# Moving side work out of two PSUM banks, and more projections ahead of the first scores, in the recurrent stage of a hybrid decoder step

## The chip, the cores and the metric

One core of a Trainium2 chip runs the kernel. The metric is the device time of one execution in microseconds; the median of the runs shown is 2340.65 us.

## What is computed

One layer of a decoder trunk serves 2048 prompt tokens and 32 sample tokens (8 sequences of 4). RMSNorm is followed by one input projection (1024 columns in, 5912 out). Branch A is sparse attention with three gated parts. Branch B is a gated linear recurrence in four heads with keys and values of 128. Both are gated, projected, merged, and added to the input. The change touches branch B alone, which is, per head and chunk:

```python
G = cumsum(log f)
o_inter = (q * exp(G)) @ S
A[t, s] = sum_d q[t, d] * exp(G[t, d] - G[s, d]) * k[s, d]      # s <= t
o = o_inter + A @ v
S = exp(G_last) * S + (k * exp(G_last - G)).T @ v
...
o = o * rsqrt(mean(o * o) + eps) * norm_g * silu(z)
```

The prompt starts from S = 0; each sample sequence has a state of its own, which is read and written back.

## The kernel before

**Projections.** `make_projections` (line 269) walks through groups of 256 columns: compressed, selected and window keys and values, then q, f, qb, ib, zb, z, ma and mb. For each group `load_w` (line 298) fetches the weights, takes their largest magnitude on VectorE (line 302), has TensorE transpose the 128 maxima of the partitions into one row of a PSUM bank (`pow2_scale`, line 197), reduces that row on VectorE (line 199), and splits the scaled weights into two 16-bit halves (lines 308 and 309). That bank is the tile `tp`, one buffer. A feature group then takes 24 matmuls for each chunk of up to 512 tokens (line 399) into one of two banks `ps`, which ScalarE and VectorE evacuate (lines 415 to 421); the late mb groups do the same at line 459 with ScalarE alone. The projections are a generator. `fill(ns)` adds to a credit and lets it emit work until the credit is used up, six matmuls of n columns costing 2.52 * n ns.

**The recurrent stage.** `hgrn` (line 645) handles 32 units, 8 chunks of 256 tokens by 4 heads, and is a generator too: `along(hgrn(), 1200.0)` runs it step by step, and after each `yield` comes `fill(1200)`. Its PSUM pools are `pa` (two banks `p4` for the scores) and `po` with one bank each of `pk`, `pu` and `ov`; with two banks of `ps` and one of `tp` all eight are given out. For a unit, `factors` loads its inputs and makes exponentials (ScalarE, VectorE, GpSimd); `scores` transposes a factor into `pk` (line 781) and multiplies the score blocks into `p4` (line 802), at high priority; `values` multiplies the chunk's contribution to the state into `pu` (line 825), the outputs into `ov` (lines 829 and 831), and VectorE makes the new state from `pu` (lines 834 and 836). When the four heads of a chunk are done, their outputs are normalized, and in each of the next four units one of them is scaled (`gate_scale`, line 683) and passes through `gate_out` (line 685): two transposes into `ov` (line 688), a multiply by the gate on VectorE that reads `ov` (line 691), a split into halves and two stores. The order in a unit's step is: scaling, factors of the unit after next, scores of the next one, gated output, values.

From the seventh unit on a step of `sample_heads` (line 849) follows each unit. A head of the samples multiplies scores into `pk` (line 873), outputs into `pu` (lines 878 and 880), transposes a factor into `pk` (line 884), and makes two products of four states each into `pu` (line 891), from which VectorE updates the states (line 896), four instructions for each product. Line 670 takes the output gates' largest magnitude through `ov` once, before the first unit.

**What sets the order.** The framework gives every instruction a priority by its place in the program, estimates times, and writes one fixed list for each engine before the run; an engine works off its list in order. Tiles of one name share the buffers of that name. Waits between engines on a buffer are semaphores that it inserts. Ahead of the loop stands the start of the stage:

```python
            ahead = [factors(*units[0])]
            for _ in range(6):
                yield
            ahead.append(factors(*units[1]))
            yield
            yield from scores(ahead[0])
```

Of the kernel before, what the change touches and what calls it, by code (L numbers as in the profile page):

```python
# [10 lines left out]
F32 = mybir.dt.float32  # L11
# [129 lines left out]
def trunk_kernel(ctx: ExitStack, tc: tile.TileContext, A, O):  # L141
# [503 lines left out]
    def hgrn():  # L645
        with ExitStack() as st:
# [3 lines left out]
            po = st.enter_context(tc.tile_pool(name="hpo", bufs=1, space=PSUM, side="right"))  # L650
# [23 lines left out]
            def rsqrt(ss):  # L674
                n = ss.shape[0]
                ve.tensor_scalar(ss, ss, 1.0 / 128, EPS, op0=OP.mult, op1=OP.add)
                y = hp.tile([128, 8], F32, name="rsy", bufs=3)[:n, :ss.shape[1]]
                ve.tensor_scalar(y, near_rsqrt(ss, hp), sob[:n], 9.0 / 64, op0=OP.mult, op1=OP.mult)
                return y

            def gate_scale(o_sb, y, nt):

                ve.tensor_tensor(o_sb, o_sb, y[:, :, None].to_broadcast([128, nt, 128]), op=OP.mult)

            def gate_out(o_sb, zt, nt, place):
                pt = po.tile([128, 512], F32, name="ov")
                for j in range(nt):
                    pe.transpose(pt[:, j * 128:j * 128 + 128], o_sb[:, j], ident)
                n = nt * 128
                g = zt  # L690
                ve.tensor_mul(g[:, :n], pt[:, :n], zt[:, :n])
                gh = hp.tile([128, NC], F16, name="gh", bufs=1)
                gl = hp.tile([128, NC], F16, name="gl", bufs=1)
                ac.activation(gh[:, :n], g[:, :n], AF.Copy)
                ve.tensor_sub(gl[:, :n], g[:, :n], gh[:, :n])
                for d, x in ((obh_d, gh), (obl_d, gl)):
                    to, x = place(d, x)
                    sy.dma_start(to, x)
# [54 lines left out]
            def factors(c, h):  # L753
                t0 = c * NC
                G, qt, kt, Bq, Bk, Xo, Kd, eG = common(h, t0, NC, 128)
                v = hp.tile([128, NJ, 128], F32, name="v", bufs=3)
                sy.dma_start(v, ib_d[t0:t0 + NC, h * 128:(h + 1) * 128].rearrange("(j p) e -> p j e", p=128))
                Xs = []
                for li, L in enumerate(LEVELS):
                    nb = NC // (2 * L)  # L760
                    Gv = G.rearrange("p (b i) -> p b i", i=2 * L)
                    ref = Gv[:, :, L - 1:L].to_broadcast([128, nb, 2 * L])
                    X = hp.tile([128, NC], F32, name=f"X{li}")
                    Xv = X.rearrange("p (b i) -> p b i", i=2 * L)

                    if nb == 2:
                        for b in range(2):
                            ac.activation(Xv[:, b], Gv[:, b], AF.Abs, scale=-1.0, bias=Gv[:, b, L - 1:L])
                    else:
                        ve.tensor_tensor(Xv, Gv, ref, op=OP.subtract)  # L770
                        ac.activation(X, X, AF.Abs)
                    ac.activation(X, X, AF.Exp, scale=-1.0)
                    gp.tensor_mul(Xv[:, :, :L], Xv[:, :, :L], kt.rearrange("p (b i) -> p b i", i=2 * L)[:, :, :L])
                    gp.tensor_mul(Xv[:, :, L:], Xv[:, :, L:], qt.rearrange("p (b i) -> p b i", i=2 * L)[:, :, L:])
                    Xs.append(X)
                return dict(Bq=Bq, Bk=Bk, Xo=Xo, Kd=Kd, eG=eG, v=v, Xs=Xs, c=c, h=h)
# [72 lines left out]
            def sample_heads():  # L849

                def zeros(name, shape):
                    t_ = hc.tile([128] + shape, F32, name=name)
                    gp.memset(t_, 0.0)
                    return t_

                for nm in ("Bk", "Kd"):
                    WIDE[nm] = zeros(nm + "_s", [128])
                v_, AT_, kd_, vm_ = zeros("vs_", [128]), zeros("ATs", [32]), zeros("kd_s", [128]), zeros("vm", [4, 128])

                oT = hc.tile([128, 4, 32], F32, name="oT")  # L860
                for h in range(4):
                    G, qt, kt, Bq, Bk, Xo, Kd, eG = common(h, 2048, 32, 4)
                    v = v_[:32]
                    sy.dma_start(v, ib_d[2048:2080, h * 128:(h + 1) * 128])
                    S0 = hp.tile([128, 8, 128], F32, name="S0", bufs=1)
                    sy.dma_start(S0, A["state_hgrn"][0, :, h].rearrange("b d e -> d b e"))

                    def masked(b2):
                        ve.tensor_tensor(vm_[:32], v[:, None].to_broadcast([32, 4, 128]), bd[:, 4 * b2:4 * b2 + 4, None].to_broadcast([32, 4, 128]), op=OP.mult)

                    masked(0)
                    pb = po.tile([128, 512], F32, name="pk")
                    mm(pb[:, :32], WIDE["Bk"], Bq, True, True)
                    AT = AT_[:32]
                    ve.tensor_mul(AT, pb[:32, :32], lm4[:32, 3])
                    yield
                    ov = po.tile([128, 512], F32, name="pu")[:, :32]
                    mm(ov, v_, AT_, True, False)
                    for b in range(8):
                        mm(ov[:, 4 * b:4 * b + 4], S0[:, b], Xo[:, 4 * b:4 * b + 4], False, True)  # L880
                    ve.tensor_copy(oT[:, h], ov)
                    yield
                    pk = po.tile([128, 512], F32, name="pk").rearrange("p (a b) -> p a b", a=4)
                    pe.transpose(pk[:, 0], WIDE["Kd"], ident)
                    kd = kd_[:32]
                    ve.tensor_copy(kd, pk[:32, 0])
                    yield
                    Sn = S0
                    for b2 in range(2):
                        pu = po.tile([128, 512], F32, name="pu").rearrange("p (a b) -> p a b", a=4)  # L890
                        mm(pu, kd_, vm_, True, True)
                        if b2 == 0:
                            masked(1)
                        for b in range(4):
                            bb = 4 * b2 + b
                            ve.scalar_tensor_tensor(Sn[:, bb], S0[:, bb], eG[:, bb:bb + 1], pu[:, b], op0=OP.mult, op1=OP.add)
                        if b2 == 0:
                            yield
                    sy.dma_start(O["s_hgrn"][0, :, h].rearrange("b d e -> d b e"), Sn)
                    yield  # L900
                pt = po.tile([128, 512], F32, name="pk")
                pe.transpose(pt[:, :128], oT.rearrange("p h t -> p (h t)"), ident)
                o_sb = hp.tile([128, NJ, 128], F32, name="o_sb", bufs=5)[:, :1]
                ss = hp.tile([128, 4 * NJ], F32, name="ss")[:, :1]
                ac.activation(o_sb[:, 0], pt[:, :128], AF.Copy)
                jk = hp.tile([128, 128], BF, name="jk", bufs=1)
                ac.activation(jk, pt[:, :128], AF.Square, accum_out=ss)
                zt = hp.tile([128, NC], F32, name="zt", bufs=6)

                def place(d, x):  # L910
                    return d[:, 2048:2080].rearrange("(h p) t -> p h t", p=128), x[:, :128].rearrange("p (h t) -> p h t", t=32)

                sy.dma_start(*place(zb_d, zt)[::-1])
                yield
                gate_scale(o_sb, rsqrt(ss), 1)
                yield
                gate_out(o_sb, zt, 1, place)

            beside = sample_heads()
            units = [(c, h) for c in range(NP // NC) for h in range(4)]  # L920

            ahead = [factors(*units[0])]
            for _ in range(6):
                yield
            ahead.append(factors(*units[1]))
            yield
# [3 lines left out]
            def gated(step):  # L930

                if ready:
                    o_sb, zt, y, h2, c2 = ready[0]
                    if step == 0:
                        gate_scale(o_sb, y, NJ)
                    else:
                        gate_out(o_sb, zt, NJ, lambda d, x: (d[h2 * 128:(h2 + 1) * 128, c2 * NC:(c2 + 1) * NC], x))
                        ready.pop(0)
# [1159 lines left out]
    with ExitStack() as s2:  # L2098
        sw, sb = ExitStack(), ExitStack()
        load_x, fill, state = make_projections(s2, sw, sb)  # L2100
# [18 lines left out]
        attention_operands(s2, att)  # L2119
        fill(0, ("zb", 2))  # L2120
        along(hgrn(), 1200.0)
        fill(0, ("z", 2))
        fill(350.0)
# [38 lines left out]
```

## Time and profile before

| | |
|---|---|
| median of the runs | 2340.65 us (2339.75 to 2341.35) |
| the profiled execution | 2322.12 us |
| its span, first to last instruction | 2320.2 us |
| its mean granted TensorE clock | 0.99 |

The trace is of one execution. Instructions are on their engines: PE is TensorE, DVE VectorE, ACT ScalarE, POOL GpSimd. Busy time counts a matmul from start to modelled end, and matmuls overlap, so TensorE's idle time says more than its busy time. A wait is charged to the instruction that stood still and to what the trace shows as ending it; "issue" means that it shows nothing.

### The profile page before, as it was taken

The page shows a single profiled execution, that of the slowest core. Times are in us where ns is not written, and L with a number is a line of the kernel's source. Part 1 is how long each engine was busy: PE and PEld are TensorE (multiplying, and loading weights), DVE is VectorE, ACT ScalarE, POOL GpSimd, SP SyncE. Part 2 cuts the span into 40 slices and gives each one's busy share as a digit, 9 for nine tenths or more (in the row PEclk, how much of TensorE's full clock was granted, in tenths as well). Part 3 has the DMA queues.
Part 4 walks back from the last instruction along what each step waited for, and adds up shares of the span by engine and source line. Part 5 has one row for each costly group of instructions (what it writes and reads, how often), then busy time and mean ns, then how long its engine had stood idle before and what let it go on. Part 6 is the DMA issues. An engine that isn't in the chain of part 4 may idle for free.

```text
span 2320.2 us, 57026 instructions
## 1 busy us (share of the span) xinstructions
PE 2215.4 (95%) x22427; PEld 1537.1 (66%) x22427; DVE 1490.3 (64%) x3780; ACT 1191.0 (51%) x2658; POOL 1005.6 (43%) x1190
## 2 busy tenths in 40 slices
PE   7999999999899989999999898999999999999998
PEld 6898775565686556665665466767667676666765
DVE  8655555756713699777753466767777676766633
ACT  7444333422622277666642366356546565667663
POOL 0100102242700066666610145457557675767763
PEclk9999999999999999999999999999999999999999
DMA  7634323677832443444335634323222121211121
GB/s 235 187 111 121 130 74 128 238 256 253 253 104 79 151 140 125 128 129 136 113 100 139 168 104 107 95 70 94 73 73 78 56 73 50 60 50 48 52 59 45
DMA packets 278388, 271.64 MB, mean 117 GB/s; under 512 B 104576, under 2 KB 248456, under 8 KB 270696
## 3 DMA queue, kind: packets, MB, share of 16 engines
q1 hardware_dynamic: 269608, 230.25, 32.6%
q0 software_dynamic: 8512, 37.75, 4.8%
q8 instruction: 176, 2.88, 0.5%
q14 instruction: 92, 0.75, 0.1%
HBM read 184.40 MB, written 87.74 MB: 117 GB/s over the span
## 4 chain that ended last, share of the span: by engine, by line
PE 71%; DVE 11%; DMA 6%; issue 4%; ACT 3%; SPq 2%; POOL 1%; POOLq 0%; DVEq 0%; ACTq 0%
PE ps L399 16%; PE ps L1926 7%; PE ps L480 7%; PE ps L1894 7%; PE ps L459 5%; PE mx L1647 3%; PE st L1783 3%; PE st L1771 3%; PE ph L1069 2%; PE po L1572 2%; PE po L1575 2%; PE po L1573 2%; PE pt L1052 1%; DMA wraw<-in_w_in_dram 1%; DVE X L770 1%
## 5 line engine op out<-in xcount | busy, mean ns | idle before, releaser
L1566 POOL TENSOR_TENSOR Pl<-P,Ph 128x512 f16<-128x512 f32 x444 | 517.9, 1176 | 335.9 <-ACT Ph L1565 202.9
L1564 ACT ACTIVATE P<-st 128x512 f32<-128x512 f32 x444 | 264.8, 597 | 243.9 <-PE st L1783 186.4
L399 PEld LDWEIGHTS <-wh 128*128 128x128 f16 x2240 | 218.2, 99 | 170.6 <-issue 19.1
L1565 ACT ACTIVATE Ph<-st 128x512 f16<-128x512 f32 x444 | 263.4, 595 | 9.9 <-PE po L1573 6.3
L399 PE MATMUL ps<-xh,wh 128*128 128x512 f16 (+1 forms) x1120 | 231.0, 342 | 7.6 <-DVE row L421 3.9
L399 PE MATMUL ps<-xl,wh 128*128 128x512 f16 (+1 forms) x1120 | 230.5, 340 | 0.0
L399 PE MATMUL ps<-xh,wl 128*128 128x512 f16 (+1 forms) x1120 | 229.8, 340 | 0.0
L1650 DVE TENSOR_REDUCE mps<-mx 128x1 f32<-128x512 f32 (+3 forms) x320 | 185.7, 603 | 51.5 <-PE mx L1647 28.0
L480 PE MATMUL ps<-wh,xh 128*128 128x256 f16 (+1 forms) x680 | 187.7, 276 | 7.6 <-ACT wh L308 4.7
L480 PE MATMUL ps<-wh,xl 128*128 128x256 f16 (+1 forms) x680 | 187.1, 275 | 1.3 <-DVE xl L365 1.3
L480 PE MATMUL ps<-wl,xh 128*128 128x256 f16 (+1 forms) x680 | 187.3, 275 | 0.0
L399 PEld LDWEIGHTS <-wl 128*128 128x128 f16 x1120 | 109.2, 98 | 80.6 <-issue 2.1
L1572 PEld LDWEIGHTS <-Ph 128*128 128x128 f16 x1776 | 141.1, 99 | 31.7 <-DVE otmp L1664 3.8
L731 POOL TENSOR_TENSOR Xo<-Xo,qt 128x256 f32<-128x256 f32 x32 | 31.7, 989 | 280.3 <-ACT Xo L730 280.3
L1573 PEld LDWEIGHTS <-Ph 128*128 128x128 f16 x1776 | 129.6, 97 | 34.3 <-issue 1.1
L480 PEld LDWEIGHTS <-xh 128*128 128x128 f16 x1360 | 130.9, 98 | 23.8 <-issue 2.9
L1650 DVE TENSOR_REDUCE mpw<-mx 128x1 f32<-128x512 f32 (+3 forms) x224 | 102.9, 483 | 43.4 <-PE mx L1649 42.0
L1894 PEld LDWEIGHTS <-xh 128*128 128x128 f16 x1280 | 104.1, 98 | 28.1 <-issue 7.5
L1575 PEld LDWEIGHTS <-Pl 128*128 128x128 f16 x1776 | 94.7, 98 | 21.5 <-POOL Pl L1566 6.3
L1572 PE MATMUL po<-vs,Ph 128*128 128x65 f16 x1088 | 106.6, 193 | 2.4 <-DVE otmp L1664 2.4
L1771 PE MATMUL st<-qb,kbs 128*128 128x512 f16 x272 | 103.6, 381 | 4.0 <-ACT Ph L1565 3.8
L1573 PE MATMUL po<-vs,Ph 128*128 128x64 f16 x1088 | 105.6, 194 | 0.0
(519 smaller groups left out, 5711.8 us busy)
## 6 DMA issues: line engine op xcount, KB each, us to landing
wraw<-in_w_in_dram SPq DMA_DIRECT2D x22, 1024.0 KB
xt<-in_x_prompt_dram SPq DMA_DIRECT2D x32, 512.0 KB
ma_d<-row SPq DMA_DIRECT2D x8, 1040.0 KB
out_y_prompt_dram<-xt SPq DMA_DIRECT2D x16, 512.0 KB
sg<-ma_d SPq DMA_DIRECT2D x56, 128.0 KB
sg<-mb_d SPq DMA_DIRECT2D x56, 128.0 KB
q_d<-row SPq DMA_DIRECT2D x4, 1040.0 KB
lf_d<-row SPq DMA_DIRECT2D x4, 1040.0 KB
```

What stands on the lines that cost most here:

```text
L399: mm(ps, l[:, kc], xs(r, t0, n)[:, kc], k == 0, k == 23)
L480: mm(ps, x, w[:, kc], k == 0, k == 23)
L1564: ac.activation(P[:n], ps, AF.Exp, scale=1.0 / QS)
L1565: ac.activation(ph[:n], ps, AF.Exp, scale=1.0 / QS)
L1566: sub.tensor_sub(pl[:n], P[:n], ph[:n])
L1572: mm(po[:, r, :w], ph[:n, rs[r]], v[:n, :w], first and r == 0, False)
L1573: mm(po[:, r, :64], ph[:n, rs[r]], v[:n, w:w + 64], False, False)
L1575: mm(po[:, r, :w], pl[:n, rs[r]], v[:n, :w], False, last)
L1650: ve.tensor_reduce(mp_[:, r, c:c + 1], pmf[:, :n], axis=AX.X, op=OP.max)
L1771: mm(ps, kb, flat(u["b"]), True, False)
L1894: mm(X["ps"], w[:, kc, cs], os_[o][:, kc], k == 0, k == 11)
L1926: mm(X["ps"], X["y"][y][:, kc, i0:i0 + r], W["o", kc // 4][w][:, kc % 4, cs], k == 0, k == 23)
```

## The change

A helper returns the bank `tp` of the projections. `gate_out` takes its transposes there instead of `ov`; the samples' outputs and state products go there instead of `pu`. At the start of the stage there are twelve steps, each followed by `fill(1200)`, in place of six.

```diff
+            def beside_units():
+
+                return state["env"]["tp"]()
+
             def gate_out(o_sb, zt, nt, place):
-                pt = po.tile([128, 512], F32, name="ov")
+                pt = beside_units()
                 for j in range(nt):
                     pe.transpose(pt[:, j * 128:j * 128 + 128], o_sb[:, j], ident)
...
                     yield
-                    ov = po.tile([128, 512], F32, name="pu")[:, :32]
+                    ov = beside_units()[:, :32]
                     mm(ov, v_, AT_, True, False)
...
                     for b2 in range(2):
-                        pu = po.tile([128, 512], F32, name="pu").rearrange("p (a b) -> p a b", a=4)
+                        pu = beside_units().rearrange("p (a b) -> p a b", a=4)
                         mm(pu, kd_, vm_, True, True)
...
             ahead = [factors(*units[0])]
-            for _ in range(6):
+            for _ in range(12):
                 yield
             ahead.append(factors(*units[1]))
```

## Rows read from the trace of the kernel before

**Rows 1.** The page, busy time, share of the span and instructions of each engine

```profile
PE 2215.4 (95%) x22427; PEld 1537.1 (66%) x22427; DVE 1490.3 (64%) x3780; ACT 1191.0 (51%) x2658; POOL 1005.6 (43%) x1190
```

**Rows 2.** Busy time by stretch: stretch, its length, busy time (instructions), granted clock, DMA share, GB/s

```profile
560.00:640.00 80.00, 66.39 (x784) 47.03 (x782) 54.55 (x96) 41.07 (x114) 47.59 (x78) 0.94 0.86 256
...
803.00:960.00 157.00, 143.96 (x1741) 92.56 (x1739) 141.79 (x313) 110.26 (x388) 99.37 (x173) 0.98 0.44 145
960.00:1165.00 205.00, 195.20 (x2303) 128.28 (x2303) 153.90 (x373) 139.16 (x492) 129.32 (x217) 1.00 0.37 115
1165.00:1240.00 75.00, 74.19 (x513) 45.07 (x514) 36.64 (x122) 26.16 (x79) 2.94 (x8) 1.00 0.35 113
1240.00:1320.00 80.00, 71.84 (x459) 40.86 (x457) 29.36 (x100) 19.02 (x29) 4.95 (x7) 0.94 0.63 156
```

**Rows 3.** TensorE's waits, 803 to 960 us: total us, times, longest

```profile
PE ov L829 <- DVE zt L691: 4.1, 3, 2.0
PE ps L399 <- DVE row L421: 3.9, 3, 2.6
```

**Rows 4.** TensorE's waits, 960 to 1240 us

```profile
PE pu L825 <- issue: 6.8, 4, 2.3
PE ov L829 <- DVE zt L691: 2.1, 2, 1.1
PE ov L688 <- DVE o_sb L683: 1.8, 1, 1.8
```

**Rows 5.** Timeline from 1064 us: start, length, engine, instruction [idle before it]

```profile
1064.48 1.02 PE L891 MATMUL pu<-vm,kd_s 128*128 128x512 f32 x2
...
1069.66 1.10 DVE L896 SCALAR_TENSOR_TENSOR S<-S,eG_s,pu 128x128 f32<-128x128 f32 x4
...
1070.87 0.35 PE L825 MATMUL pu<-v,kd 128*128 128x128 f32 x1 [2.32 <-issue]
```

**Rows 6.** Timeline around 867 us, VectorE's row and then TensorE's

```profile
866.92 0.41 DVE L691 TENSOR_TENSOR zt<-ov,zt 128x256 f32<-128x256 f32 x1
...
867.39 0.49 PE L829 MATMUL ov<-v,AT 128*128 128x128 f32 x2 [2.02 <-DVE zt L691]
```

**Rows 7.** Timeline at the first unit's score tile, its state product, the output gates' maxima

```profile
607.45 0.63 DVE L816 COPY_PREDICATED AT<-lmi,own 128x128 f32<-128x128 int32 x1
...
636.53 0.39 PE L825 MATMUL pu<-v,kd 128*128 128x128 f32 x2
...
803.40 0.27 PE L222 MATMUL ov<-ident,mxs 128*128 128x128 f32 x1
```

**Rows 8.** Timeline from 1134 us, TensorE's rows and then VectorE's

```profile
1134.74 1.02 PE L891 MATMUL pu<-vm,kd_s 128*128 128x512 f32 x2
...
1137.57 0.38 PE L688 MATMUL ov<-ident,o_sb 128*128 128x128 f32 x2
...
1139.23 1.10 DVE L896 SCALAR_TENSOR_TENSOR S<-S,eG_s,pu 128x128 f32<-128x128 f32 x4
```

**Rows 9.** Timeline of one weight group's maxima: the reduction, and the transpose that follows

```profile
936.91 2.29 DVE L302 TENSOR_REDUCE wmx<-wraw 128x1 f32<-128x2048 f32 x1 [0.72 <-DMA wraw<-in_w_in_dram]
...
989.49 0.27 PE L197 MATMUL tp<-ident,wmx 128*128 128x128 f32 x1
```

**Rows 10.** TensorE's waits, 560 to 640 us

```profile
PE tp L197 <- DVE wmx L302: 3.2, 1, 3.2
```

**Rows 11.** Groups by line on TensorE, 803 to 1240 us: count | busy us, mean ns | idle

```profile
L688 PE MATMUL ov<-ident,o_sb 128*128 128x128 f32 x65 | 14.3, 288 | 3.4 <-DVE o_sb L683 3.4
...
L197 PE MATMUL tp<-ident,wmx 128*128 128x128 f32 x7 | 1.9, 273 | 0.0
```

**Rows 12.** Busy time by stretch, early in the recurrent stage, columns as in rows 2

```profile
840.00:860.00 20.00, 15.87 (x161) 10.40 (x147) 19.20 (x40) 13.59 (x39) 8.57 (x16) 0.91 0.33 113
860.00:880.00 20.00, 17.98 (x247) 11.34 (x246) 19.75 (x45) 15.36 (x56) 14.92 (x24) 0.91 0.46 149
```

**Rows 13.** Timeline: the first scores; the splitting of the z projections' first weights

```profile
591.99 0.27 PE L802 MATMUL p<-X 128*32 128x32 f32 x8
...
799.72 2.34 DVE L309 SCALAR_TENSOR_TENSOR wl<-wraw,wxs,wh 128x2048 f16<-128x2048 f32 x1
```

## The prediction

> **What bounds the kernel now.** The first view is the page's busy table: TensorE has a matmul in flight for 95% of the span, VectorE follows with 64% [rows 1]. So the time falls only where TensorE stands idle, or runs at the lower clock. The second view, busy time by stage, says where that is. The recurrent stage's matmuls lie among projections from 560 to 1240 us, and I cut there by what each stretch does [rows 2]. From 560 to 640 us TensorE idles 13.6 of 80 us; the first four units are worked ahead there. From 803 to 960 us it idles 13.0 of 157, with VectorE busy for 142 of 157: the stage's dense beginning, where VectorE is close to being the limit. From 960 to 1165 us it idles 9.8 of 205, and VectorE has room (154 of 205). From 1165 to 1240 us it idles 0.8 of 75. From 1240 to 1320 us, where the prompt phase begins, it idles 8.2 of 80 at a granted clock of 0.94.
>
> The third view, TensorE's waits, names the idle time. From 803 to 960 us: 4.1 us in three waits of the values' matmul (line 829) for the multiply of the gated output (line 691), and 3.9 us for a projection's evacuation on VectorE [rows 3]. From 960 to 1240 us: 6.8 us in four waits before the state product (line 825), put down to "issue"; 2.1 us in two more waits of line 829 for line 691; and 1.8 us for the scaling at line 683, which the change doesn't touch [rows 4].
>
> "Issue" hides a bank. In the timeline the samples' product into `pu` starts at 1064.48; the four state updates that read that bank run on VectorE from 1069.66 to 1070.76; and line 825, whose tile is also `pu`, starts at 1070.87 after 2.32 us idle [rows 5]. The other four-update groups end in the same way just before the other three waits. The waits of line 829 are the same thing on `ov`: the multiply that reads the gated output's transposes out of `ov` runs from 866.92 to 867.33, and the values' product into `ov` starts at 867.39 [rows 6]. So 6.2 + 6.8 = 13.0 us of idle time come from two banks, each shared between the chain of units and something beside it. These are what the change takes apart.
>
> **The change, part by part.** No instruction is added or removed: 65 transposes of gated outputs [rows 11] and the samples' twelve groups of products (three for each of four heads) are written to another bank.
>
> 1. `ov` without gated outputs. Bounds 0 to 6.2 us. The two late waits (2.1 us) lie where VectorE has room, and I count them whole. Of the three early ones (4.1) I count half: there VectorE is 90% busy [rows 2], and TensorE, let go earlier, meets the next result that VectorE owes it (a projection's evacuation, row two of [rows 3]). Gain 4.1 us.
>
> 2. `pu` without the samples' products. Bounds 0 to 6.8 us. Line 825 then waits only for the previous unit's two state updates. I count all of it: 6.8 us.
>
> 3. New waits on `tp`. Its order is now gated output, samples' product, gated output, with a weight group's maximum in between. Is a bank given out in the order of the program? Unit 0's first score tile was final at 608.08 and its `v` had been used at 636.53, yet its values' product stayed behind the output-gate scale, which took `ov` first and reached TensorE at 803.40 [rows 7]. So yes: on `tp` each user waits for the reader of the one before it. From below this costs nothing: the list order of TensorE is made knowing it, with other matmuls in between. From above, in the old order the next gated transposes follow the samples' product by 2.83 us (1134.74 to 1137.57), while the updates that read it end at 1140.33 [rows 8]; met unprepared, that is 2.8 us at each of the eight products of line 891, 22 us. What TensorE meets in a list made beforehand is only the lateness of VectorE, and the four waits on `pu` are its measure: 1.7 us each, at four of eight products. I take three of 1.7: a loss of 5.1 us. The Trainium skill, PSUM — Partial Sum Buffer, "PSUM bank collisions raise a hardware error", speaks against the change here: its rule is to "Semaphore-guard PSUM by bank × quadrant", not by address, so three users of different columns still exclude each other. By that rule alone, with the old order, item 3 would be the 22 us; [rows 5] show such waiting within one bank, and no row shows two engines in one bank at once.
>
> 4. The weights' maxima share `tp` too, seven of them from 803 to 1240 us [rows 11]. The reduction of one ended at 939.20 and its transpose came at 989.49, when its place in TensorE's list came up [rows 9]; that 50 us cover a shift of a few us, and I cost it at nothing. If that cover goes, TensorE stands still as it did before such a transpose earlier on, for 3.2 us [rows 10]; that is a rival below. The gated outputs' DMAs and the SP queue shift by as little: nobody reads those rows before the merge, and a fifth `o_sb` buffer gives one unit's slack.
>
> 5. The clock. Between 840 and 880 us the granted clock was 0.91 [rows 12], a mean of 2.4 GHz and, for some 7 us after TensorE had waited, 1.2 GHz: a loss of 0.09 x 40 = 3.6 us; the stretch holds the 2.0 us wait of [rows 6] and idle time that stays. I count a quarter: gain 0.9 us.
>
> 6. Twelve fills instead of six. Six more of 1200 ns put 7.2 us of projections ahead of the first scores in priority. In the trace the first scores ran at 591.99, long before the weights of the projections in question were split, at 799.72 [rows 13]; so nothing can come ahead of these scores in time, and what moves is the order after 803 us: projections win against values and later units. It takes 7.2 us of projections out of the later stages, where they were filler, so the work itself gains nothing. From below: nothing, or a loss if the recurrent stage ends 7.2 us later against its filler; from 1165 to 1240 us TensorE has 0.8 us idle [rows 2], so filler is there. From above: the 3.9 us that TensorE waits for evacuations early on [rows 3], whose VectorE work now comes first. I take a third: gain 1.3 us.
>
> Sum: 4.1 + 6.8 - 5.1 + 0.9 + 1.3 = 8.0 us. The profiled execution took 2322.1 us (span 2320.2 and 1.9 around it), so 2314.1 by its own time; the median of the runs is 18.5 us above it, and I move that by the same amount: 2340.65 - 8.0 = 2332.6 us. About 0.2%, 4.7 us, is what a measurement can tell here.
>
> **The rivals.**
> A. The wait only changes its place: `tp` costs what `pu` gave back (6.8 instead of 5.1), the early `ov` waits come back whole as waits for evacuation (gain 2.1), no clock, no gain from item 6. Then 2.1 us remain: 2338.5 us. For it: VectorE's 90% early on, and the short distance in [rows 8]. Against it: the longest `pu` wait, the 2.3 us of [rows 5], has no gated transposes near it that it could move to.
> B. Slower: a weight group's maximum stops TensorE. Its place is `tp`; a gated output or a samples' product behind it waits for its raw weights, or it for them, and TensorE's list stands still as in [rows 10]. Price 3.2 us for each of seven loads, 22.4 us, less the 13.0 gained: 2350 us. It decides from the fifth load on (13.0 / 3.2 = 4.1). Against it: the 50 us between reduction and transpose in [rows 9].
> C. The change does not do what its words say: nothing is put ahead of the first scores (item 6). Then item 6 is zero, 2333.9 us, inside the forecast.
> D. More than forecast: no new wait on `tp`, all of 13.0, all of item 5's 1.8 for 860 to 880 us: 2326 us.
> E. The new order also moves the start of the prompt phase, which loses 8.2 us idle and 0.06 x 80 = 4.8 us of clock now [rows 2], by a few us either way. It is no case of its own but widens the range.
>
> **How the numbers follow.** Forecast with C: 0.46. D: 0.10. A: 0.28. B, with the bad side of E: 0.16. Faster by over 0.2% (below 2336.0) is forecast and D, 0.56; within 0.2% is A, 0.28; slower 0.16. The likeliest case gives 2332.6, by itself 2328 to 2336. The range takes in D with 1.5 us of E below, and A with 5 us of E above: 2324.5 to 2343.5. B is left out.
>
> **What would show it.** In the changed kernel's waits from 960 to 1240 us, no "issue" before line 825 and nothing at line 829 for line 691; instead some 5 us before line 688 (waiting for line 896) or lines 878 and 891 (waiting for line 691). TensorE's idle time from 803 to 1165 us falls from 22.8 to about 15 us. VectorE's busy time stays. The forecast is wrong if line 688 or line 197 shows over 10 us of waits, or if TensorE's idle time is the same with line 399 waiting for evacuations, or if the stretch after 1165 us changes by more than the stretch before it.

## The result, and the profile after

The changed kernel takes 2328.36 us (median of six runs, 2320.94 to 2329.66), the kernel before 2340.79 us (six runs, 2339.39 to 2346.2). The ratio is 0.9945, with an interval of 0.9928 to 0.9962: faster by 12.4 us of the medians. The forecast was 2332.6 us with a gain of 8.0. Sign, size and range held; the place of the gain did not, and most of this section and the next is about that. All ratios in this document are those on record, which are not quotients of the medians and differ from these by up to 0.0005.

The page of the changed kernel, its span, its busy line (see [rows 1]) and its granted clock:

```profile
span 2327.1 us, 57011 instructions
PE 2221.2 (95%) x22427; PEld 1542.1 (66%) x22427; DVE 1490.2 (64%) x3780; ACT 1194.3 (51%) x2658; POOL 1006.0 (43%) x1190
PEclk9999999999899999999999999999999999999999
```

The first thing to see is a contradiction: this span is longer than the 2320.2 us of the execution that the prediction read, though the medians fell. That execution was a lucky one before the change begins to matter. Its output gates' maxima (line 222) ran at 803.4 us; in the thirteen other traces of this study they ran between 811.8 and 820.6 us, though the changed kernel's lists are those of the kernel before up to there (TensorE's first difference comes at 809.8 us in the first trace of before). So times before line 222 tell nothing of the change, and from here on every time is counted from line 222 (+437 is 437 us behind it). The kernel before was traced a second time for a fair partner; that run is called the second trace of before.

Busy time by stage, cut at line 222, +437 and +517, in the changed kernel (the window, its length, busy us of TensorE, weight load, VectorE, ScalarE and GpSimd with counts, granted clock, DMA share, GB/s):

```profile
819.10:1256.10 437.00, 416.81 (x4570) 269.33 (x4569) 331.81 (x807) 278.70 (x960) 233.44 (x397) 0.99 0.40 127
1256.10:1336.10 80.00, 78.28 (x495) 43.12 (x494) 29.02 (x89) 22.84 (x32) 4.62 (x4) 1.00 0.69 184
```

The same cut in the second trace of before:

```profile
813.00:1250.00 437.00, 413.58 (x4559) 266.65 (x4558) 332.39 (x805) 275.22 (x959) 232.58 (x397) 0.99 0.39 125
1250.00:1330.00 80.00, 71.06 (x456) 40.35 (x455) 29.64 (x100) 19.36 (x29) 4.62 (x4) 0.94 0.62 156
```

The recurrent stage (the first 437 us) lost 3.2 us of its idle time: 23.4 before, 20.2 after (18.5 in the second trace of the changed kernel). The next 80 us, where the prompt phase begins, lost 7.2: 8.9 before, 1.7 after, the clock rose from 0.94 to 1.00, and 39 more matmuls found room (495 against 456). This is the stretch of the last row of [rows 2], of which the prediction said that it was no case of its own.

TensorE's waits in the recurrent stage of the changed kernel (what stood still, what ended it, us in all, count, the longest), which answer to [rows 3] and [rows 4]:

```profile
PE ps L399 <- DVE row L421: 6.0, 4, 3.2
PE tp L692 <- DVE S L900: 3.1, 2, 2.1
PE tp L692 <- DVE o_sb L683: 3.1, 4, 1.2
PE tp L197 <- DVE S L900: 2.8, 1, 2.8
PE p L806 <- DVE each L818: 1.3, 2, 1.0
PE ov L835 <- DVE S L840: 1.3, 2, 0.7
PE tp L692 <- DVE zt L695: 1.3, 1, 1.3
PE tp L895 <- DVE zt L695: 1.0, 1, 1.0
...
```

From line 685 on the lines of the changed kernel stand 4 further down (829 became 833, 825 became 829, 688 became 692). The waits of line 829 for the gated output and the four "issue" waits of line 825 are gone, as forecast. In their place stand four rows on `tp` that end with a reader of `tp` at line 900 or 695. The three before a gated output or a samples' product hold 3.1 + 1.3 + 1.0 = 5.4 us, where item 3 of the forecast had 5.1. The fourth, 2.8 us before a weight group's maxima (line 197), is what item 4 put at nothing. Evacuations (line 399 for line 421) hold 6.0 us, where [rows 3] had 3.9, and lines 835 and 806 now wait 1.3 us each for VectorE. The Trainium skill, PSUM — Partial Sum Buffer, "PSUM bank collisions raise a hardware error", asks for a guard by bank and quadrant (32 partitions), not by address; the users of `tp` all write from column 0 on, so they overlap by address too, and no run here tells the one kind of guard from the other.

**Where the time went.** Idle time is a poor measure of matmuls that overlap: a late one can shorten the overlap and show no idle time at all (in the rows below, groups of line 459 last 1.89 us and start 1.73 us apart). (The Trainium skill, Trainium Kernel Development and Optimization, "Performance Expectations", says that matmul busy time is a bad metric for how close a kernel is to the roofline, because matmuls are pipelined. Placing a few microseconds is another use of it; here the idle time of the recurrent stage fell by 3.2 us, the time lost by the measure below by 1.5.) So I took for each matmul the gap from its start to the next start, less the usual gap of its line and shape (the 30th percentile over two traces, one of each kernel), and summed the rest as lost time. Between line 222 and the end, us:

| trace | recurrent, 0 to +437 | prompt start, +437 to +577 | +577 to +1000 | +1000 to end | line 222 to end |
|---|---|---|---|---|---|
| before, first | 48.5 | 12.6 | 24.2 | 27.0 | 1516.8 |
| before, second | 48.1 | 13.3 | 27.6 | 26.8 | 1520.1 |
| after, first | 45.7 | 2.2 | 27.9 | 27.8 | 1508.0 |
| after, second | 47.8 | 1.7 | 26.7 | 26.7 | 1507.4 |

By the means of two traces the tail shrank by 1518.5 - 1507.7 = 10.8 us. The recurrent stage gave 48.3 - 46.8 = 1.5 of it, where idle time had shown 3.2; the start of the prompt phase gave 13.0 - 2.0 = 11.0; the rest took 1.7 back, 1.4 of it in the third column. The 1.5 us are not clear of the spread, since the two traces of the changed kernel differ by 2.1 there; the 11.0 are. (The cut at +577 matters: the last projections end at +585 in the changed kernel and at +616 in the one before, and the loss that follows in both would fall on two sides of a cut between these.)

**What happens there.** The timeline of TensorE and VectorE around the start of the prompt phase, in the kernel before (start and duration in us, engine, line, operation, xcount of those that follow each other; in brackets the idle time ahead and what ended it):

```profile
1229.94 2.29 DVE L302 TENSOR_REDUCE wmx<-wraw 128x1 f32<-128x2048 f32 x1 [3.72 <-DMA wraw<-in_w_in_dram]
...
1289.74 1.89 PE L459 MATMUL ps<-xh,wl 128*128 128x512 f16 x8
...
1293.96 0.22 PE L1572 MATMUL mx<-vc,Ph 128*128 128x97 f16 x1 [2.12 <-ACT Ph L1565]
...
1299.12 0.45 PE L1714 MATMUL mx<-ident,repp 128*128 128x128 f32 x1 [3.17 <-DVE repp L1710]
...
1299.36 0.42 PE L197 MATMUL mx<-ident,wmx 128*128 128x128 f32 x1
...
1305.77 1.89 PE L459 MATMUL ps<-xh,wh 128*128 128x512 f16 x8
```

A block of the prompt phase begins with a chain: scores, exponentials on ScalarE (`Ph`), a product (line 1572), a selection of the largest on VectorE (`repp`), a transpose (line 1714). The waits above are those of the second block. What TensorE could do meanwhile are the last projections (line 459). But those of the last weight group can't start, since the group's maxima are transposed (line 197, on the bank `mx` at this stage) only at 1299.36, behind the chain, though VectorE had reduced them at 1229.94. From the group that starts at 1289.74 to the one at 1305.77 there is no matmul of line 459, and TensorE stands still for 2.1 and 3.2 us. The same in the changed kernel, second trace:

```profile
1296.75 0.28 PE L197 MATMUL mx<-ident,wmx 128*128 128x128 f32 x1
...
1301.40 1.89 PE L459 MATMUL ps<-xh,wh 128*128 128x512 f16 x8
1303.13 1.89 PE L459 MATMUL ps<-xl,wh 128*128 128x512 f16 x8
1304.86 1.89 PE L459 MATMUL ps<-xh,wh 128*128 128x512 f16 x8
1306.58 0.38 PE L459 MATMUL ps<-xl,wh 128*128 128x512 f16 x1
1306.80 0.21 PE L1576 MATMUL mx<-vc,Ph 128*128 128x97 f16 x1
```

Here the maxima are transposed ahead of the second block's chain, and line 459 fills the time ahead of line 1576 (1572 before) without a gap. The weights did not arrive earlier for it: VectorE reduces the last group's maxima at +445.0 in this trace and at +426.5 in the first of before (1229.94 above). What moved is the place of line 197 in TensorE's list. The weights of the last group are split (line 309) at +484.5 in this trace and +482.9 in the first, against +502.3 and +502.7 in the two of before.

### The profile page after: what moved, and what is told of

Read it like the earlier page. It is cut to its first block, busy times and chain, and to the rows that moved or that the text cites. A ratio compares the mean times of both kernels' runs of the same rounds, so it can differ in the third digit from the quotient of the medians.

```text
span 2327.1 us, 57011 instructions
## 1 busy us (share of the span) xinstructions
PE 2221.2 (95%) x22427; PEld 1542.1 (66%) x22427; DVE 1490.2 (64%) x3780; ACT 1194.3 (51%) x2658; POOL 1006.0 (43%) x1190
## 4 chain that ended last, share of the span: by engine, by line
PE 71%; DVE 11%; DMA 6%; issue 4%; ACT 3%; SPq 1%; POOL 1%; another core or an unknown queue 0%; POOLq 0%; ACTq 0%; DVEq 0%
PE ps L399 17%; PE ps L1930 8%; PE ps L1898 7%; PE ps L480 7%; PE ps L459 6%; PE mx L1651 3%; PE st L1787 3%; PE st L1775 3%; PE ph L1073 2%; PE po L1576 2%; PE po L1579 2%; PE po L1577 2%; DMA wraw<-in_w_in_dram 2%; DVE X L774 2%; PE pt L1056 1%
## 5 line engine op out<-in xcount | busy, mean ns | idle before, releaser
L399 PE MATMUL ps<-xl,wh 128*128 128x512 f16 (+1 forms) x1120 | 235.9, 342 | 0.1
```

The costliest lines, as they stand in the source:

```text
L399: mm(ps, l[:, kc], xs(r, t0, n)[:, kc], k == 0, k == 23)
```

## The experiments

The theories that the expectations number are these. First: the bank waits in the recurrent stage are the gain (the prediction's). Second: the gain is a new order of the projections behind 1240 us, and, once the first batch was in, that it takes both parts of the change together. Third: every variant is a draw of the order. Fourth: the last weight group comes in time to fill the start of the prompt phase. Fifth: the recurrent tail ends some 22 us earlier, and that is the gain. Ratios are to the kernel before on the same chip.

**One part at a time.** Both bank moves with the old count of steps:

```diff
-            for _ in range(12):
+            for _ in range(6):
```

> Both bank moves, six steps as before. Theory 1 (the waits on the two banks are the gain): 8 to 11 us faster than before, about 2330 to 2333 us, and from the output gates' maxima (line 222) to the end some 1508 us as in the changed kernel (1508.0) against 1516.8 before; TensorE waits before line 829 for line 695 and before the state product gone. Theory 2 (the new order of projections after 1240 us is the gain, and the bank waits only changed place): within 4 us of before, the stretch from 617 to 1000 us after line 222 idle for some 11.7 us as before, not 7.3.

The kernel before with twelve steps and its own banks:

```diff
-            for _ in range(6):
+            for _ in range(12):
```

> Twelve steps, banks as before. Theory 1: within 3 us of before (about 2339 us), the waits of line 829 for line 691 and of line 825 for line 896 still there, some 13 us in all. Theory 2: 5 to 10 us faster than before, with the gain later than 1240 us in the trace.

The kernel before with the gated outputs alone on `tp`:

```diff
-                pt = po.tile([128, 512], F32, name="ov")
+                pt = state["env"]["tp"]()
```

> Only the gated outputs' transposes on tp. Theory 1: the 6.2 us of waits of line 829 for line 691 go, the 6.8 us before line 825 stay: 3 to 6 us faster than before. Theory 2: within 3 us of before.

And with the samples alone on `tp`:

```diff
-                    ov = po.tile([128, 512], F32, name="pu")[:, :32]
+                    ov = state["env"]["tp"]()[:, :32]
...
-                        pu = po.tile([128, 512], F32, name="pu").rearrange("p (a b) -> p a b", a=4)
+                        pu = state["env"]["tp"]().rearrange("p (a b) -> p a b", a=4)
```

> Only the samples' products on tp. Theory 1: the 6.8 us of waits before line 825 go, nothing new on tp since only seven weight maxima share it: 5 to 8 us faster than before. Theory 2: within 3 us of before.

Measured:

| kernel | median us | ratio, interval | last split (line 309) at | lost: recurrent | lost: prompt start |
|---|---|---|---|---|---|
| both banks, six steps | 2336.33 | 0.9996, 0.9985 to 1.0006 | +500.4 | 47.8 | 12.6 |
| twelve steps, old banks | 2336.46 | 0.9996, 0.9984 to 1.0008 | +492.8 | 50.0 | 16.3 |
| gated outputs alone | 2334.09 | 0.9984, 0.9973 to 0.9995 | +498.9 | 48.1 | 10.6 |
| samples alone | 2332.10 | 0.9975, 0.9964 to 0.9986 | +502.6 | 51.6 | 10.6 |

(The kernel before had a median of 2338.33 here.) Neither half of the change is worth anything that can be told from nothing: 0.9996 both times, with room for 3.7 us at most, against 0.9945 together (0.9933 on this chip, below). That is against the prediction's theory, by which both banks with six steps should have kept nearly all: from line 222 to the end their trace took 1518.5 us, not 1508. It is against the second theory in its first form too, by which twelve steps alone should have gained 5 to 10 us. The bank waits did go in that kernel, and others came. TensorE's waits of both banks with six steps, recurrent stage and then prompt start:

```profile
PE ps L399 <- DVE row L421: 8.2, 5, 3.7
PE tp L692 <- DVE o_sb L683: 4.4, 5, 1.8
PE ov L835 <- DVE S L840: 3.2, 2, 2.0
PE tp L197 <- DVE zt L695: 1.7, 1, 1.7
...
PE mx L1718 <- DVE repp L1714: 3.3, 2, 2.5
PE st L1691 <- ACT qc L1562: 2.1, 1, 2.1
```

VectorE's debts take the place of the banks: evacuations 8.2 us (3.9 in [rows 3]), the scaling of line 683 4.4 (3.4 in [rows 11]), the state update of line 840 3.2. And the chain of the prompt start still meets TensorE without filler (line 1718, which is 1714 before). With twelve steps and the old banks, the recurrent stage keeps its waits, and the prompt start has others:

```profile
PE pu L825 <- issue: 8.4, 5, 2.8
PE ov L829 <- DVE zt L691: 4.5, 5, 1.5
...
PE mx L1647 <- DVE qs L1715: 6.8, 1, 6.8
PE ps L459 <- ACT piece L464: 4.0, 2, 3.5
```

The single bank moves gained 0.16 and 0.25%, and the two together 0.04%. By the medians, 4.2 and 6.2 us, the single moves gained what the first theory expects of them (3 to 6 and 5 to 8); but their traces lost 48.1 and 51.6 us in the recurrent stage, no less than before, so the number held without its cause. Parts that don't add up speak for the third theory as far as such small differences go.

**Repeats, and other counts.** The kernel before and the changed one again, and the changed one with 11 and with 14 steps (`range(11)`, `range(14)`).

> The kernel before itself, for a second trace of it: ratio 1.000. The time from the output gates' maxima (line 222) to the end was 1516.8 us in its first trace. Theory 1 and 2 need it to stay within 3 us of that; if it differs by 5 us or more with the same order of instructions, single traces can't place a gain of this size.

> The changed kernel once more, on the chip of the runs before. If the 0.9945 is the kernel's and not the first chip's, it is 10 to 14 us faster than before again, about 2326 us where before has 2338, though both of its parts alone (both banks with six steps; twelve steps alone) measured 0.9996. Theory 2 (both parts are needed together) and theory 3 (every variant gets a newly made order of instructions, and its time is a draw with several us of spread) both expect that; a ratio near 0.999 would say that the first result was the chip's.

> Both bank moves with eleven steps in place of twelve: 1.2 us of projections less ahead of the first scores. Theory 2 (the amount of projections ahead matters beside the banks): within 3 us of the changed kernel, ratio to before 0.994 to 0.996. Theory 3 (a draw of the order): as likely near before, ratio 0.997 to 1.002.

> Both bank moves with fourteen steps: 2.4 us more of projections ahead. Theory 2: within 3 us of the changed kernel, ratio 0.994 to 0.996. Theory 3: anywhere from 0.994 to 1.002.

Measured, with a median of 2337.8 us for the kernel before: itself again 2335.93 (0.9992, 0.9982 to 1.0002), with 1520.1 us from line 222 to the end, 3.3 more than in its first trace where 3 were allowed; the changed kernel again 2321.76 (0.9933, 0.9921 to 0.9945); eleven steps 2321.71 (0.9932, 0.9918 to 0.9945); fourteen 2327.81 (0.996, 0.9945 to 0.9974). Lost time in the recurrent stage and at the prompt start: 43.5 and 1.7 us with eleven, 42.5 and 7.1 with fourteen. So twelve is no lucky draw, as far as one neighbour can show it: eleven gives the same, by the same gain at the prompt start (1.7 us, like the changed kernel's 2.2 and 1.7). In the recurrent stage eleven and fourteen lose 4.8 and 5.8 us less than before, where the changed kernel loses 1.5 less. Fourteen lose 5 us of that again, and by the medians they are 6.1 us slower than eleven. TensorE's waits at the prompt start, second trace of before:

```profile
PE mx L1714 <- DVE repp L1710: 3.2, 1, 3.2
PE mx L1572 <- ACT Ph L1565: 2.8, 1, 2.8
PE ps L459 <- ACT piece L464: 2.5, 1, 2.5
PE mx L1575 <- POOL Pl L1566: 0.4, 1, 0.4
```

They are 8.9 us. In the second trace of the changed kernel one wait is left there:

```profile
PE ps L459 <- ACT piece L464: 1.2, 1, 1.2
```

**The last weights' time.** Is it the late split of the last group that leaves the chain without filler? In the loop of the late groups the last group's fetch can be moved by a chunk. Earlier, on the kernel before, on both banks with six steps, and on the changed kernel:

```diff
             for c in range(6):
+                if c == 0:
+                    fetch(late[3][1])
                 if c < 5:
                     yield from gate(*late[2][1:], *CHUNKS[c])
-                if c == 0:
-                    fetch(late[3][1])
-                else:
+                if c > 0:
```

> The kernel before, with nothing of the change; only the weights of the last mb group are fetched one chunk earlier in the program (10 us of projections). Theory 4 (the gain is the last group's weights arriving in time to fill the start of the prompt phase): TensorE's loss between 437 and 517 us after line 222 falls from 13 us to under 5, ratio to before 0.994 to 0.997. Theory 5 (the gain is that the recurrent stage's tail ends 22 us earlier with the bank moves, the weights being a bystander): within 0.2% of before, ratio 0.998 to 1.002.

> Both bank moves, six steps, and the last mb group's weights one chunk earlier. Theory 4: as fast as the changed kernel or faster, ratio 0.992 to 0.996, though the same without the early fetch measured 0.9996. Theory 5: like both bank moves with six steps, 0.998 to 1.002.

> The changed kernel with the last mb group's weights one chunk earlier. Theory 4: they are in time already, so within 4 us of the changed kernel, ratio to before 0.991 to 0.995. Theory 5: the same.

And a chunk later, on the changed kernel:

```diff
-                if c == 0:
+                if c == 1:
                     fetch(late[3][1])
-                else:
+                if c > 0:
```

> The changed kernel, all three parts kept, with the last mb group's weights fetched one chunk later. Theory 4: the gain is lost, the stall between 437 and 517 us after line 222 is back at 8 us or more, ratio to before 0.997 to 1.001. Theory 5: the gain stays, 0.992 to 0.995.

Measured, with a median of 2343.62 us for the kernel before:

| kernel | median us | ratio, interval | last split (line 309) at | lost: recurrent | lost: prompt start |
|---|---|---|---|---|---|
| before, early fetch | 2341.96 | 0.9993, 0.9985 to 1.0002 | +480.7 | 49.3 | 12.8 |
| banks, six steps, early | 2335.40 | 0.9964, 0.9950 to 0.9978 | +482.8 | 49.6 | 5.2 |
| changed, early | 2328.08 | 0.9933, 0.9920 to 0.9946 | +470.3 | 45.6 | 2.4 |
| changed, late | 2336.49 | 0.9973, 0.9962 to 0.9984 | +505.0 | 46.0 | 16.3 |

The late fetch is the sharpest of the twelve. One line moved by one chunk puts the split at +505.0, and 0.27% are left of the 0.67% that the changed kernel gained in its second measurement, on another chip, and gains here with the early fetch. Its windows, recurrent stage and prompt start, beside the changed kernel's above:

```profile
818.70:1255.70 437.00, 417.61 (x4569) 269.75 (x4568) 331.86 (x807) 279.02 (x960) 233.97 (x397) 0.98 0.40 127
1255.70:1335.70 80.00, 70.95 (x443) 39.75 (x441) 29.04 (x97) 18.08 (x27) 4.62 (x4) 0.91 0.59 148
```

The recurrent stage is the changed kernel's (417.6 us busy against 416.8), the prompt start is that of before (71.0 against 71.1 busy, and 1.00 of granted clock has become 0.91). Its waits there are the old ones, four lines further down:

```profile
PE mx L1718 <- DVE repp L1714: 2.7, 1, 2.7
PE mx L1576 <- ACT Ph L1569: 2.1, 2, 1.4
PE ps L459 <- ACT piece L464: 2.1, 1, 2.1
PE mx L1579 <- POOL Pl L1570: 0.6, 1, 0.6
...
```

The fifth theory falls by this run: the tail ends as early as in the changed kernel (last line 688 at +410.7), and most of the gain is gone. So that the last group's maxima come in time is needed. What sets it can be read from the order of TensorE's matmuls on the bank `mx`. In every other kernel with eleven steps or more, and in those with the early fetch, line 197 stands ahead of the second block's products (line 1572); in the kernel before, in the three with six steps and moved banks, and with the late fetch it stands behind that block's transposes (line 1714), and all of these lose 10.6 us or more at the prompt start. So the steps and the fetch decide its place, and the banks don't.

The place is not enough either, and the fourth theory alone falls in its turn: the kernel before with the early fetch has its split at +480.7, as early as the changed kernel, and gains nothing. Its waits from +437 to +528:

```profile
PE ps L459 <- ACT piece L464: 4.0, 2, 2.8
PE mx L1647 <- DVE mpw L1650: 3.4, 1, 3.4
```

The filler is there, but now it is ScalarE's evacuation (line 464) and another reduction (line 1650) for which TensorE waits. What VectorE waits for there shows best with twelve steps and the old banks, where it holds TensorE's 6.8 us before line 1647 (ScalarE's row, then VectorE's):

```profile
1335.86 1.15 ACT L1841 ACTIVATE xh<-wraw,swa 128x1024 f16<-128x1024 f32 x1 [8.51 <-DMA wraw<-in_w_branch_a_dram]
...
1337.04 1.28 DVE L1842 SCALAR_TENSOR_TENSOR xl<-wraw,swa,xh 128x1024 f16<-128x1024 f32 x1 [8.56 <-ACT xh L1841]
...
1340.99 0.68 DVE L1715 TENSOR_SCALAR qs<-mx 32x512 f16<-32x512 f32 x1
```

The splitting of the weights `w_branch_a` for the merge (lines 1841 and 1842) stands ahead of the chain's step (line 1715) in VectorE's list, and these weights come late. With the early fetch alone ScalarE waits 9.5 us for the same weights, in the two traces of the changed kernel 1.0 and 0.9. With the bank moves added to the early fetch the prompt start's loss falls from 12.8 to 5.2, and with the twelve steps to 2.4.

**What this settles.** The early fetch adds nothing to the changed kernel (0.9933 and 0.9933), so it has that gain already. No kernel tried is clearly faster than the changed one. What stays open is how the bank moves help the prompt start. They end the recurrent tail earlier: the last gated transposes (line 688) come at +410.5 and +412.6 in the changed kernel, at +408.6 with both banks and six steps, and at +408.9 and +416.7 with one bank moved, against +432.4 and +432.0 before. By itself that gives little: with the gated outputs alone the split still comes at +498.9. The last split, at +502.5 before by the mean of two traces, came 2.1 us earlier with the banks alone, 9.7 with the twelve steps alone, and 18.8 with both; why it is more than the sum was not tried apart, and that with the place of line 197 right an earlier end of the tail lets the merge's weights come sooner is only argued. Also open: the late fetch keeps 0.27% by its median (seven runs), while its one trace, which was its slowest run (2341.35 us), shows a tail as long as that of before. The four traces of the changed kernel and its two fetch variants have a mean of 46.3 us lost in the recurrent stage (45.7, 47.8, 45.6, 46.0), 2.0 less than before; that places a third of the 6 us left, and the rest is not placed.

## Why the prediction was right and wrong

The time was right: 2332.6 forecast, 2328.36 measured, inside the likeliest case's own 2328 to 2336. The cause was right in its first half only, and that the number held is luck: the stage that was to give 8.0 us gave 1.5, and one that was left out of the sum gave 11.0.

1. Items 1 and 2, the two banks. Right that both waits go: none of the 6.2 and 6.8 us is left. Wrong in what follows: TensorE met VectorE's next debts, at line 399 (6.0 us against 3.9), at lines 835 and 806 (1.3 each), and on `tp`; at line 683 it waits as before (3.1 against 3.4). The prediction allowed for that in half of the three early waits and counted the two late ones and all of `pu` whole.
2. Item 3, `tp`. Right in kind and size: the waits of lines 692 and 895 for readers of `tp` are 5.4 us in the first trace of the changed kernel and 2.1 + 1.3 + 1.0 = 4.4 in the second, against 5.1. The 22 us of its upper bound are far off. (Its "different columns" is a misreading of the kernel: all users begin at column 0.)
3. Item 4, the weights' maxima. Costed at nothing, measured 2.8 and 2.7 us in the two traces, one wait of line 197 each (the second is put down to VectorE's line 217). That is one, not the seven of rival B, which fell.
4. Item 5, the clock. Wrong sign in the recurrent stage: 6.8 us at the lower of the two clocks there before, 10.2 in the first trace of the changed kernel and 20.5 in the second. The clock was won back at the prompt start instead, 0.94 to 1.00 over 80 us.
5. Item 6, the steps. The 1.3 us were to come off the 3.9 that line 399 waits for evacuations. With the old banks twelve steps made that wait longer, 5.5 us; with both banks moved they made it shorter, 8.2 with six and 6.0 with twelve. What the steps do beside that, the place of the last group's maxima at the prompt start, is not in the item.
6. The sum put 8.0 us into the recurrent stage, and its idle time from 803 to 1165 us was to fall from 22.8 to 15. It gave 1.5 us (3.2 of idle time). The step that failed is rival E: "It is no case of its own but widens the range." That stretch gave 11.0 us. The text held its price already, 8.2 us idle and 4.8 of clock [rows 2], and asked only whether the start moves, not what TensorE lacks there. The last row of the stretch, and the weights of the last group behind the chain, would have shown it in the trace of before, if not that this change removes it: line 302 at 1229.94 and line 197 at 1299.36.
7. The text named its own test: the forecast is wrong "if the stretch after 1165 us changes by more than the stretch before it". By that test it is, though its number held. Rival A, that the wait only changes its place, is nearly what happened in the recurrent stage.

The sum was read from an execution 18.5 us faster than the median, and moved by that difference. The traces bear this out in the main: of the 12.9 us between the two profiled executions of before, 9.6 lie ahead of line 222, which the change can't move, and 3.3 behind it.

## What to carry to other kernels

Where a kernel's matmuls are fillers for each other, look for the places where the filler runs out, and for what lets the next filler start (here a weight group whose maxima wait behind a chain that needs the filler); here 13.0 us of waits removed elsewhere gave 1.5. A removed wait can come back as the next one where a second engine is nearly as busy (here VectorE, 90% at the stage's beginning): count the second engine's debts first. Trace both kernels twice, count times from the last instruction that the change can't move, and measure matmuls from start to start.

## What the runs showed of the hardware

The same instructions took between 803.4 and 820.6 us up to line 222 in the fourteen traces, a spread larger than the gain under study, and only in that part; behind it the two traces of each kernel agree within 3.3 and 0.6 us. And where the prompt start is broken up by a few waits of 2 to 3 us, the clock was lower as well: in the second trace of before TensorE ran for 10.2 us at 1.2 GHz from +491, behind the chain's waits, and with the late fetch for 10.2 us from +490; in the two traces of the changed kernel, without those waits, it stayed at 2.4 GHz there.
